# A two-layer encoder trunk: 28 projections stream the high and low halves of h side by side as 512 columns

## The chip, the cores and the metric

The kernel runs on one core of a Trainium2 chip. The metric is device time in microseconds, the median of several runs of the same program. TensorE does matrix products and writes PSUM; VectorE (DVE) and ScalarE (ACT) read and write SBUF and PSUM; GpSimd (POOL) does a few masks and roots; the DMA issues all stand in SyncE's queue (SP). Each engine takes its instructions strictly in the order in which they are written, and waits on semaphores of the others.

## The reference, cut to what matters

Each of two layers normalises x (256 rows of 1024), projects it by one wide matrix whose columns feed three branches, and merges the branches:

```
h = rmsnorm(x, norm_w)
proj = einsum('bld,de->ble', h, w_in)
(fq, fk, fv, ff, fg, sz, sxbc, sdt, dq, dk, dv, dg, mg) = split(proj)
y_a = forgetting_attention(fq, fk, fv, log_f) * silu(fg)
xbc = silu(causal_depthwise_conv(sxbc, conv_w, conv_b))   # 4 taps over time, by channel
y_b = rmsnorm(ssd_scan(xbc ...) * silu(sz)) * ssm_norm_w
y_c = rmsnorm(differential_attention(rope(dq), rope(dk), dv)) * silu(dg)
merged = sum over branches of sigmoid(mg) * (branch @ w_branch)
x = x + merged @ w_out
```

All of it is in float32. The kernel keeps that precision by writing each operand of a large product as the sum of two fp32r numbers, a high half and a low half, and adding three products: high by high, high by low, and low by high.

## The kernel before, in words

**Weights.** The columns are cut into chunks of 512 (`chunk_list`), each loaded as 4 units of 128 partitions by 1024 (two 128-row tiles k of 512 columns). `load_chunk` brings a unit in as `raw`; ScalarE casts it to `whi` (L231), VectorE subtracts to get `wlo` (L232). `whi` and `wlo` have 8 buffers each, so two chunks: the units of a chunk can only be split once TensorE has used up the same units two chunks earlier. A chunk is requested about two chunks ahead of its use.

**Two forms of product.** In the B form (`bform`, L249) h, or the output of a branch, is the stationary operand and the weights stream past, 512 columns at a time; the result has time on its partitions. In the A form (`aform`, L264) the weights are stationary and h streams past; the result has channels on its partitions and the 256 time steps along the bank. 14 chunks of each layer go in the A form: fq, fk and fg (two each, attention A), sB, sC, sx0, sx1 (the convolved part of branch B), dq and dk (two each, branch C). An A bank of 512 columns holds two tiles of 128 channels by 256 steps; for each of the 8 k-tiles and each of the two channel tiles there are three matmuls of 256 columns, with `whi` and the high half of h, `whi` and the low half, `wlo` and the high half.

**Emptying a bank.** `pp` has 3 PSUM banks for the large products. Each A chunk has a function that empties its bank: `t_evac` splits q and k straight from PSUM for the score products; `g_evac` computes u·(1+tanh(u/2)) from PSUM; `r_evac` copies dq and dk out with ScalarE (L766); `c_evac` copies with ScalarE into `sw` (L784), then ScalarE scales by the last tap (L470), VectorE adds three taps for each 128-channel tile (L473), ScalarE takes a tanh into the same buffer (L787) and VectorE multiplies (L788).

**Order.** Small pieces of the attention and the scan are jobs that `pump` places between the banks. The instructions of every engine are then ordered at compile time by a scheduler that follows priorities (earlier in the program first) and the buffers that are free; so the order on each engine is fixed before the run. `ap` is the pool of general SBUF buffers of 128 by 512, 41 of them; the halves of h take 8.

Of the kernel before, what the change touches and what calls it, by code (L numbers as in the profile page):

```python
# [24 lines left out]
KT = D // P  # L25
UNITS = 4
KU = KT // UNITS
# [69 lines left out]
def trunk(ctx: ExitStack, tc: tile.TileContext, x, norm_w, weights, small, vectors,  # L97
          final_norm_w, rope_t, out):
    nc = tc.nc
    V, S, G, PE = nc.vector, nc.scalar, nc.gpsimd, nc.tensor  # L100
# [1 line left out]
    const = ctx.enter_context(tc.tile_pool(name="const", bufs=1))  # L102
    wraw = ctx.enter_context(tc.tile_pool(name="wraw", bufs=4))
    wsp = ctx.enter_context(tc.tile_pool(name="wsp", bufs=8))
    ap = ctx.enter_context(tc.tile_pool(name="ap", bufs=41))
    sp = ctx.enter_context(tc.tile_pool(name="sp", bufs=5))
    tp = ctx.enter_context(tc.tile_pool(name="tp", bufs=2))
    sm = ctx.enter_context(tc.tile_pool(name="sm", bufs=2))
# [7 lines left out]
    def a2(shape=None, dtype=F32):  # L116
        return ap.tile(shape or [P, 2, 256], dtype, name="a2")
# [4 lines left out]
    def halves():  # L122
        return tuple([a2(dtype=F32R) for _ in range(4)] for _ in range(2))

    def at(half, kt):
        return half[kt // 2][:, kt % 2, :]

    def bank(pool, name):
        return pool.tile([P, 512], F32, name=name)
# [83 lines left out]
    chunks, _ = chunk_list()  # L213
# [36 lines left out]
                      start=((u, k, i) == order[0]), stop=((u, k, i) == order[-1]))  # L250
        return ps

    def aform(ch, act, jj):
        units, n = ch
        ahi, alo = act
        ps = bank(pp, "pp")
        for u in range(UNITS):
            whi, wlo = units[u]
            for k in range(KU):
                kt = u * KU + k  # L260
                for j in range(2):
                    c0 = (2 * jj + j) * P
                    for i, (w, a) in enumerate(((whi, ahi), (whi, alo), (wlo, ahi))):
                        PE.matmul(ps[:, j * T:(j + 1) * T], lhsT=w[:, k, c0:c0 + P], rhs=at(a, kt),  # L264
                                  start=(kt == 0 and j == 0 and i == 0), stop=(kt == KT - 1 and j == 1 and i == 2))
        return ps

    scr_x = dr.tile([2, P, D], F32, name="scr_x")
    L = [dict() for _ in range(DEPTH)]

    def make_h(l, tt, xt, xs, ss, gap):
        st = L[l]
        if tt == 0:
            st["hT"] = halves()
        with tc.high_priority(URGENT):
            r = norm_scale(ss)
            for c in range(2):
                norm_apply(xt, xs, r, st["nwb"], c)
        yield gap
        with tc.high_priority(URGENT):  # L280
            for c in range(2):
                st["split"] = split_rows(xs[c], st["hT"][0], st["hT"][1], tt, c)
        st[f"h{tt}"] = True
# [106 lines left out]
    def split_qk(key, src):  # L390
        tiles = [a2(dtype=F32R) for _ in range(2 if key[1] == "q" else 4)]
        (stack_q if key[1] == "q" else stack_k)(src, tiles)
        return tiles
# [323 lines left out]
    def plan(l):  # L717
        st = L[l]
# [36 lines left out]
            return f  # L755

        def t_evac(key):
            def f(jj, ps):
                st[f"{key[0:2]}{2 * int(key[2]) + jj}"] = split_qk(key, ps.rearrange("p (a t) -> p a t", t=T))
            return f  # L760

        def r_evac(key):
            def f(jj, ps):
                t = a2()
                st.setdefault("_" + key, []).append(t)
                S.copy(out=t, in_=ps.rearrange("p (a t) -> p a t", t=T))  # L766
                if jj == 1 and key[:2] == "dk":
                    start_job(rope, l, int(key[2]))
            return f

        def g_evac(key):
            def f(jj, ps):
                t = a2()
                p3 = ps.rearrange("p (a t) -> p a t", t=T)
                S.activation(out=t, in_=p3, func=AF.Tanh, scale=0.5)
                V.scalar_tensor_tensor(out=t, in0=t, scalar=1.0, in1=p3, op0=ALU.add, op1=ALU.mult)
                st[f"{key[0:2]}{2 * int(key[2]) + jj}"] = t
            return f

        def c_evac(key, j0):  # L780
            def f(jj, ps):
                t = a2()
                u = tp.tile([P, 2, T], F32, name="sw")
                S.copy(out=u, in_=ps.rearrange("p (a t) -> p a t", t=T))  # L784
                for i in range(2):
                    conv_tile(l, u[:, i, :], t[:, i, :], j0 + 2 * jj + i)
                S.activation(out=u, in_=t, func=AF.Tanh)  # L787
                V.scalar_tensor_tensor(out=t, in0=u, scalar=1.0, in1=t, op0=ALU.add, op1=ALU.mult)  # L788
                st.setdefault("_" + key, []).append(t)
                if jj == 1:  # L790
                    st[key] = st["_" + key]
            return f

        def merge(tt):
            if tt == 0:
# [159 lines left out]
    for idx, it in enumerate(items):  # L955
# [28 lines left out]
        for s in range(2):  # L984
            for (_, _, ch), ev in zip(got, it["evac"]):
                if it["kind"] == "A":
                    ev(s, aform(ch, it["act"](), s))
                else:
                    while f"{it['flag']}{s}" not in L[l]:
                        pump(100.0)  # L990
                    ev(s, bform(ch, it["act"](), s))
                pump(BUDGET)
# [27 lines left out]
```

## Time and profile before

| | |
|---|---|
| median of 3 runs | 955.47 us (955.02 to 956.32) |
| the profiled execution | 956.56 us, of which the span of the trace is 954.8 us |
| busy in the span | TensorE 942.0 us, weight loads 843.5 us, VectorE 700.9 us, ScalarE 599.3 us |
| share of the last-ending chain | TensorE 98% |

Busy time of an engine is the time in which an instruction of it is under way; matmuls overlap, so the mean duration of one is longer than the distance from one to the next. What a matmul costs in a stream is read from the chain in order of time, as length by count. The granted clock is given as a share of full speed, 1.00 for 2.4 GHz. Sums below are made against the profiled execution, 1.09 us over the median.

### The profile page before, as it was taken

Reading aid. Unit: us, or ns where it says so; the run is one execution under the profiler, and the core shown is the slowest. Engines: PE = TensorE matmul, PEld = TensorE weight load, DVE = VectorE, ACT = ScalarE, POOL = GpSimd, SP = SyncE. Lnnn points to the kernel's source line nnn. Section 1 sums busy time; section 2 is a strip of 40 time slices with the busy share of each in tenths; the row PEclk is TensorE's granted clock in tenths of the full one; section 3 lists DMA queues with packets and bytes.
Section 4 is the critical chain, followed back from the end, with each engine's and each line's share of the span. In section 5 each row is a group of like instructions: output and inputs, shape, how many; then the busy total and the mean of one; then the engine's idle time right before and its main releaser. Section 6 shows DMA issues by size and latency. Waiting matters only on the chain.

```text
span 954.8 us, 16246 instructions
## 1 busy us (share of the span) xinstructions
PE 942.0 (99%) x5924; PEld 843.5 (88%) x5924; DVE 700.9 (73%) x1434; ACT 599.3 (63%) x1141; POOL 36.3 (4%) x71
## 2 busy tenths in 40 slices
PE   7999999999999999999999999999999999999997
PEld 5999999988898988888889989898889999888885
DVE  5678677987667877864768768699777677797463
ACT  4668686654557868653546859566536596975442
POOL 1001100000000000100000110000000000010000
PEclk7999999999999999999999999999999999999999
DMA  6866634575555555555558664456645555555551
GB/s 231 263 219 198 206 101 166 159 226 154 177 189 181 182 190 179 151 171 194 193 181 271 209 206 134 132 172 191 201 143 194 174 186 186 188 158 162 177 188 44
DMA packets 60319, 172.45 MB, mean 181 GB/s; under 512 B 7312, under 2 KB 15824, under 8 KB 60240
## 3 DMA queue, kind: packets, MB, share of 16 engines
q1 hardware_dynamic: 60240, 171.43, 55.4%
q8 instruction: 46, 0.75, 0.3%
q14 instruction: 33, 0.27, 0.1%
HBM read 167.14 MB, written 2.16 MB: 177 GB/s over the span
## 4 chain that ended last, share of the span: by engine, by line
PE 98%; DMA 1%; DVE 1%; ACT 0%; SPq 0%; POOLq 0%; issue 0%
PE pp L249 51%; PE pp L264 34%; PE pq L400 2%; PE pt L457 2%; PE pq L583 1%; PE pq L401 1%; PE pq L447 1%; DMA raw<-in_weights_dram 1%; PE pt L627 1%; PE pt L198 1%; PE pt L458 1%; PE pq L692 1%; PE pq L590 0%; PE pt L700 0%; PE pq L499 0%; PE pt L699 0%
## 5 line engine op out<-in xcount | busy, mean ns | idle before, releaser
L249 PE MATMUL pp<-whi,a 128*128 128x512 f32 (+1 forms) x1472 | 452.5, 387 | 1.9 <-ACT a L188 1.1
L232 DVE TENSOR_TENSOR wlo<-raw,whi 128x1024 fp32r<-128x1024 f32 (+1 forms) x296 | 349.8, 1193 | 82.8 <-ACT whi L231 80.0
L231 ACT CAST whi<-raw 128x1024 fp32r<-128x1024 f32 (+1 forms) x296 | 302.2, 1027 | 135.2 <-PE pp L249 72.3
L264 PE MATMUL pp<-a,whi 128*128 128x256 f32 x1792 | 332.8, 284 | 0.0
L249 PEld LDWEIGHTS pp<-whi,a 128*128 128x128 f32 x1472 | 273.0, 189 | 55.3 <-ACT a L188 1.7
L264 PEld LDWEIGHTS pp<-a,whi 128*128 128x128 f32 x1792 | 281.5, 191 | 1.7 <-issue 1.4
L249 PE MATMUL pp<-wlo,a 128*128 128x512 f32 (+1 forms) x736 | 281.5, 385 | 0.0
L264 PE MATMUL pp<-a,wlo 128*128 128x256 f32 x896 | 255.2, 285 | 0.0
L264 PEld LDWEIGHTS pp<-a,wlo 128*128 128x128 f32 x896 | 171.5, 191 | 1.4 <-issue 1.4
L249 PEld LDWEIGHTS pp<-wlo,a 128*128 128x128 f32 x736 | 138.9, 189 | 25.8 <-DVE wlo L232 0.5
L183 POOL TENSOR_TENSOR rstd<-rstd,mhalf 128x2 f32<-128x2 f32 (+2 forms) x26 | 18.9, 727 | 760.6 <-DVE rstd L181 739.7
L473 DVE SCALAR_TENSOR_TENSOR a<-sw,pT,a 128x255 f32<-128x255 f32 (+2 forms) x96 | 41.8, 477 | 8.1 <-ACT a L470 7.9
L406 ACT ACTIVATE sc<-sc,dnm 128x128 f32<-128x128 f32 x64 | 28.6, 450 | 8.4 <-DVE dnm L403 8.3
L188 ACT CAST a<-pt 128x256 fp32r<-128x256 f32 x32 | 11.5, 371 | 33.2 <-PE pt L198 27.0
L400 PE MATMUL pq<-a,a 128*128 128x128 f32 (+1 forms) x128 | 31.8, 283 | 0.0
L809 DVE SCALAR_TENSOR_TENSOR a<-a,pp 128x512 f32<-128x512 f32 x24 | 16.4, 682 | 20.9 <-PE pp L249 20.9
L401 PE MATMUL pq<-a,a 128*128 128x128 f32 (+1 forms) x128 | 31.5, 269 | 0.0
L406 ACT ACTIVATE sc<-sc,nm 128x128 f32<-128x128 f32 (+1 forms) x64 | 28.5, 447 | 1.3 <-DVE nm L403 1.1
L400 PEld LDWEIGHTS pq<-a,a 128*128 128x128 f32 x128 | 23.7, 191 | 0.3
L401 PEld LDWEIGHTS pq<-a,a 128*128 128x128 f32 x128 | 23.6, 191 | 0.3
L403 DVE CUSTOM_DVE_ANT_0 sc<-pq,sc 128x128 f32<-128x128 f32 (+1 forms) x64 | 19.5, 351 | 5.9 <-POOL sc L426 4.9
L191 ACT ACTIVATE a<-pt,pT 128x256 fp32r<-128x256 f32 x32 | 14.9, 473 | 14.1 <-PE pt L627 12.4
(161 smaller groups left out, 842.6 us busy)
## 6 DMA issues: line engine op xcount, KB each, us to landing
raw<-in_weights_dram SPq DMA_DIRECT2D x280, 512.0 KB, 4.5
raw<-in_weights_dram SPq DMA_DIRECT2D x16, 272.0 KB, 3.5
sc<-scr SPq DMA_DIRECT2D x16, 256.0 KB, 5.5
a<-scr SPq DMA_DIRECT2D x16, 256.0 KB, 5.6
a<-in_x_dram SPq DMA_DIRECT2D x8, 256.0 KB, 5.2
sc<-scr SPq DMA_DIRECT2D x16, 128.0 KB, 5.2
a<-in_norm_w_dram SPq DMA_DIRECT2D x4, 256.0 KB, 6.5
rp<-a SPq DMA_DIRECT2D x32, 32.0 KB, 4.1
```

The source lines that it names most:

```text
L183: G.tensor_tensor(out=r[:, 0:width], in0=r[:, 0:width], in1=mhalf[:, 0:width], op=ALU.pow)
L231: S.copy(out=hi, in_=raw)
L232: V.tensor_tensor(out=lo, in0=raw, in1=hi.bitcast(F32), op=ALU.subtract)
L249: PE.matmul(ps[:, 0:n], lhsT=at(a, kt)[:, ts], rhs=w[:, k, 0:n], start=((u, k, i) == order[0]), stop=((u, k, i) == order[-1]))
L264: PE.matmul(ps[:, j * T:(j + 1) * T], lhsT=w[:, k, c0:c0 + P], rhs=at(a, kt), start=(kt == 0 and j == 0 and i == 0), stop=(kt == KT - 1 an ...
L400: PE.matmul(ps[:, o:o + n], lhsT=q[:, j, qs], rhs=k[:, j, 0:n], start=True, stop=False)
L401: PE.matmul(ps[:, o:o + n], lhsT=q[:, j, qs], rhs=kl[:, j, 0:n], start=False, stop=True)
L403: V.tensor_tensor_reduce(out=sc[:, sl], in0=ps[:, sl], in1=bias[:, sl], scale=-0.125, scalar=BIG, op0=ALU.add, op1=ALU.min, accum_out=nm[: ...
L406: S.activation(out=sc[:, sl], in_=sc[:, sl], func=AF.Exp, scale=-1.0, bias=nm[:, t:t + 1], accum_out=rs[:, t:t + 1])
L457: PE.matmul(po[r, 0:T], lhsT=v0, rhs=pTs[i][:, 0:T], start=True, stop=False)
L473: V.scalar_tensor_tensor(out=xc[:, s:T], in0=u[:, 0:T - s], scalar=pr["conv"](j, k), in1=xc[:, s:T], op0=ALU.mult, op1=ALU.add)
L809: V.scalar_tensor_tensor(out=t, in0=t, scalar=1.0, in1=ps, op0=ALU.add, op1=ALU.mult)
```

## The change

h's halves move from 8 buffers of `ap` into one tile `hboth`, where for each k-tile the 256 high columns and the 256 low columns lie side by side. An A bank now belongs to one tile of 128 channels: for each k-tile one matmul of 512 columns (`whi` against both halves) and one of 256 columns (`wlo` against the high half, added to the first half of the bank). The two halves of a finished bank are added by the new `fold`: ScalarE copies the second half to SBUF, VectorE adds the first half to it and writes one half of a pair buffer `u` (two buffers) or, for dq and dk, of a buffer of `ap`. After two banks the old work on a pair starts, reading the pair buffer in SBUF. The copies L766 and L784 go. `ap` shrinks from 41 to 30 buffers.

```
-    ap = ctx.enter_context(tc.tile_pool(name="ap", bufs=41))
+    ap = ctx.enter_context(tc.tile_pool(name="ap", bufs=30))
...
+    hboth = ctx.enter_context(tc.tile_pool(name="hp", bufs=1)).tile([P, KT, 2, T], F32R, name="hboth")
+    h_halves = tuple([hboth[:, 2 * i:2 * i + 2, s, :] for i in range(4)] for s in range(2))
...
-    def aform(ch, act, jj):
+    def aform(ch, j):
...
-                for j in range(2):
-                    c0 = (2 * jj + j) * P
-                    for i, (w, a) in enumerate(((whi, ahi), (whi, alo), (wlo, ahi))):
-                        PE.matmul(ps[:, j * T:(j + 1) * T], lhsT=w[:, k, c0:c0 + P], rhs=at(a, kt),
-                                  start=(kt == 0 and j == 0 and i == 0), stop=(kt == KT - 1 and j == 1 and i == 2))
+                kt, cols = u * KU + k, slice(j * P, (j + 1) * P)
+                PE.matmul(ps, lhsT=whi[:, k, cols], rhs=hboth[:, kt], start=(kt == 0), stop=False)
+                PE.matmul(ps[:, 0:T], lhsT=wlo[:, k, cols], rhs=hboth[:, kt, 0, :],
+                          start=False, stop=(kt == KT - 1))
...
+    def fold(ps, dst):
+        t = tp.tile([P, T], F32, name="fold")
+        S.copy(out=t, in_=ps[:, T:2 * T])
+        V.tensor_tensor(out=dst, in0=ps[:, 0:T], in1=t, op=ALU.add)
+
+    def raw_pair():
+        return tp.tile([P, 2, T], F32, name="u")
+
+    def folded(f, new=raw_pair):
+        pair = []
+
+        def g(j, ps):
+            if j % 2 == 0:
+                pair.append(new())
+            fold(ps, pair[-1][:, j % 2, :])
+            if j % 2:
+                f(j // 2, pair[-1])
+        return g
...
         def r_evac(key):
-            def f(jj, ps):
-                t = a2()
-                st.setdefault("_" + key, []).append(t)
-                S.copy(out=t, in_=ps.rearrange("p (a t) -> p a t", t=T))
+            def f(jj, u):
+                st.setdefault("_" + key, []).append(u)
...
-            return f
+            return folded(f, a2)
...
         def c_evac(key, j0):
-            def f(jj, ps):
+            def f(jj, u):
                 t = a2()
-                u = tp.tile([P, 2, T], F32, name="sw")
-                S.copy(out=u, in_=ps.rearrange("p (a t) -> p a t", t=T))
...
-                    ev(s, aform(ch, it["act"](), s))
+                    for j in (2 * s, 2 * s + 1):
+                        ev(j, aform(ch, j))
```

`t_evac` and `g_evac` are wrapped in `folded` in the same way and read `u` where they read the bank.

TensorE, inside an A bank of the kernel before (`a_152` and `a_149` are high halves of h, `a_156` and `a_153` low ones):

```order
228 L264 MATMUL pp<-a_152,whi 128x256
229 L264 MATMUL pp<-a_156,whi 128x256
230 L264 MATMUL pp<-a_152,wlo 128x256
231 L264 MATMUL pp<-a_152,whi 128x256
232 L264 MATMUL pp<-a_156,whi 128x256
233 L264 MATMUL pp<-a_152,wlo 128x256
```

The same work in the changed kernel, where L263 and L264 are the two matmuls of the new `aform`:

```order
112 L263 MATMUL pp<-hboth,whi 128x512
113 L264 MATMUL pp<-hboth,wlo 128x256
114 L263 MATMUL pp<-hboth,whi 128x512
115 L264 MATMUL pp<-hboth,wlo 128x256
116 L263 MATMUL pp<-hboth,whi 128x512
```

Three matmuls of 256 columns have become one of 512 and one of 256, and the two pairs of rows belong to the same bank where they belonged to two halves of it.

VectorE in layer 1 of the kernel before, at the first convolved chunk (sB): the taps of two pairs, with the splits of the weights that come two chunks later.

```order
850 L473 SCALAR_TENSOR_TENSOR a_7129<-sw,pT_3119,a_7129 128x255 x2
851 L473 SCALAR_TENSOR_TENSOR a_7129<-sw,pT_3119,a_7129 128x254 x2
852 L473 SCALAR_TENSOR_TENSOR a_7129<-sw,pT_3119,a_7129 128x253 x2
853 L788 SCALAR_TENSOR_TENSOR a_7129<-sw,a_7129 128x512
854 L473 SCALAR_TENSOR_TENSOR a_7215<-sw,pT_3119,a_7215 128x255 x2
855 L473 SCALAR_TENSOR_TENSOR a_7215<-sw,pT_3119,a_7215 128x254 x2
856 L232 TENSOR_TENSOR wlo<-raw,whi 128x1024
857 L473 SCALAR_TENSOR_TENSOR a_7215<-sw,pT_3119,a_7215 128x253 x2
858 L232 TENSOR_TENSOR wlo<-raw,whi 128x1024 x3
859 L788 SCALAR_TENSOR_TENSOR a_7215<-sw,a_7215 128x512
```

VectorE at the second and third convolved pairs of layer 1 in the changed kernel (`a_6747` and `a_6823` are their results; L492 are the taps, L802 the products, L235 the splits of weights, L271 the folds, L481 an attention output). Ahead of these rows stand the two folds that complete the pair of `a_6823`, then seven taps and one product of attention A.

```order
918 L492 SCALAR_TENSOR_TENSOR a_6747<-u,pT_2939,a_6747 128x253 x2
919 L492 SCALAR_TENSOR_TENSOR a_6823<-u,pT_2939,a_6823 128x254
920 L235 TENSOR_TENSOR wlo<-raw,whi 128x1024
921 L492 SCALAR_TENSOR_TENSOR a_6823<-u,pT_2939,a_6823 128x253
922 L235 TENSOR_TENSOR wlo<-raw,whi 128x1024
923 L481 TENSOR_TENSOR a_5447<-sc,a_5443 128x256
924 L492 SCALAR_TENSOR_TENSOR a_6823<-u,pT_2939,a_6823 128x253
925 L235 TENSOR_TENSOR wlo<-raw,whi 128x1024 x2
926 L802 SCALAR_TENSOR_TENSOR a_6747<-u,a_6747 128x512
927 L802 SCALAR_TENSOR_TENSOR a_6823<-u,a_6823 128x512
928 L271 TENSOR_TENSOR u<-pp,fold 128x256 x2
```

Where no instruction of VectorE stood between the end of a bank and its release before (ScalarE's copy freed it), the release of the next bank, the fold in row 928, now stands in VectorE's queue behind the taps of two pairs, four splits and two products.

## Rows read from the trace of the kernel before

**Rows 1.** The page: busy time, share of the span and instructions by engine.

```profile
PE 942.0 (99%) x5924; PEld 843.5 (88%) x5924; DVE 700.9 (73%) x1434; ACT 599.3 (63%) x1141; POOL 36.3 (4%) x71
```

**Rows 2.** The page: the chain that ended last, by engine.

```profile
PE 98%; DMA 1%; DVE 1%; ACT 0%; SPq 0%; POOLq 0%; issue 0%
```

**Rows 3.** The chain in order of time: start, length (us), what, how many.

```profile
237.52 24.75 PE pp L249 x109
...
262.27 17.27 PE pp L264 x144
```

**Rows 4.** Groups by shape, A-form matmuls: count | busy us, mean ns | idle before.

```profile
L264 PE MATMUL pp<-a,whi 128*128 128x256 f32 x1792 | 332.8, 284 | 0.0
...
L264 PE MATMUL pp<-a,wlo 128*128 128x256 f32 x896 | 255.2, 285 | 0.0
```

**Rows 5.** Groups by shape: copies and additions of the sizes that come and go.

```profile
L189 DVE TENSOR_TENSOR a<-pt,a 128x256 fp32r<-128x256 f32 x32 | 13.1, 419 | 11.7 <-ACT a L188 11.5
L188 ACT CAST a<-pt 128x256 fp32r<-128x256 f32 x32 | 11.5, 371 | 33.2 <-PE pt L198 27.0 <-DVE a L189 6.2
...
L766 ACT COPY a<-pp 128x512 f32<-128x512 f32 x16 | 9.3, 582 | 11.3 <-PE pp L264 11.1
...
L784 ACT COPY sw<-pp 128x512 f32<-128x512 f32 x16 | 9.3, 580 | 17.6 <-PE pp L264 17.3
```

**Rows 6.** Busy us by engine in four stretches, then granted clock, DMA share.

```profile
138.00:186.00 48.00, 48.00 (x381) 45.66 (x380) 40.05 (x68) 31.70 (x48) 0.00 (x0) 1.00 0.43 139
...
186.00:210.00 24.00, 24.00 (x119) 20.21 (x118) 23.64 (x51) 13.27 (x21) 0.00 (x0) 1.00 0.78 238
210.00:262.00 52.00, 52.00 (x255) 43.75 (x254) 36.99 (x69) 24.94 (x43) 1.02 (x1) 1.00 0.55 169
507.00:650.00 143.00, 143.00 (x1167) 137.28 (x1166) 113.57 (x262) 102.18 (x198) 7.67 (x16) 1.00 0.53 177
```

**Rows 7.** VectorE's timeline: start, length, instruction, count [idle before].

```profile
592.60 2.36 DVE L232 TENSOR_TENSOR wlo<-raw,whi 128x1024 fp32r<-128x1024 f32 x2
...
615.84 2.45 DVE L473 SCALAR_TENSOR_TENSOR a<-sw,pT,a 128x255 f32<-128x255 f32 x6
619.04 0.69 DVE L788 SCALAR_TENSOR_TENSOR a<-sw,a 128x512 f32<-128x512 f32 x1 [0.76 <-ACT sw L787]
```

**Rows 8.** Waits in 138 to 186 us: us in total, times, longest.

```profile
ACT sw L784 <- PE pp L264: 6.4, 2, 3.6
ACT whi L231 <- PE pp L264: 5.8, 10, 2.4
DVE a L473 <- ACT a L470: 3.9, 3, 1.8
...
DVE wlo L232 <- ACT whi L231: 1.6, 2, 1.2
DVE a L788 <- ACT sw L787: 0.8, 1, 0.8
```

**Rows 9.** Timeline of the start, ScalarE and TensorE.

```profile
14.17 0.37 ACT L188 CAST a<-pt 128x256 fp32r<-128x256 f32 x1 [0.54 <-DVE a L189]
14.44 1.99 ACT L231 CAST whi<-raw 128x1024 fp32r<-128x1024 f32 x2
...
15.54 2.08 PE L249 MATMUL pp<-whi,a 128*128 128x512 f32 x4 [0.80 <-ACT whi L231]
16.33 0.42 ACT L942 ACTIVATE a<-a 128x256 f32<-128x256 f32 x1
```

**Rows 10.** Busy us by engine at the start, then granted clock, DMA share.

```profile
0.00:15.50 15.50, 9.62 (x38) 7.45 (x38) 5.33 (x13) 5.49 (x12) 2.36 (x14) 0.83 0.77 280
15.50:41.00 25.50, 25.43 (x148) 22.73 (x149) 18.37 (x36) 17.23 (x36) 0.56 (x1) 0.90 0.69 212
```

More of the change, by code (lines that the diff above doesn't have):

```diff
@@ L251, in bform @@
         return ps
-    def aform(ch, act, jj):
+    def aform(ch, j):
         units, n = ch
-        ahi, alo = act
         ps = bank(pp, "pp")
@@ L259, in aform @@
             for k in range(KU):
-                kt = u * KU + k
-                for j in range(2):
-                    c0 = (2 * jj + j) * P
-                    for i, (w, a) in enumerate(((whi, ahi), (whi, alo), (wlo, ahi))):
-                        PE.matmul(ps[:, j * T:(j + 1) * T], lhsT=w[:, k, c0:c0 + P], rhs=at(a, kt),
-                                  start=(kt == 0 and j == 0 and i == 0), stop=(kt == KT - 1 and j == 1 and i == 2))
-        return ps
+                kt, cols = u * KU + k, slice(j * P, (j + 1) * P)
+                PE.matmul(ps, lhsT=whi[:, k, cols], rhs=hboth[:, kt], start=(kt == 0), stop=False)
+                PE.matmul(ps[:, 0:T], lhsT=wlo[:, k, cols], rhs=hboth[:, kt, 0, :],
+                          start=False, stop=(kt == KT - 1))
+        return ps
+    def fold(ps, dst):
[13 more added lines that the diff above has]
+        return g
     scr_x = dr.tile([2, P, D], F32, name="scr_x")
@@ L273, in make_h @@
         if tt == 0:
-            st["hT"] = halves()
+            st["hT"] = h_halves
         with tc.high_priority(URGENT):
@@ L757, in t_evac, with f @@
         def t_evac(key):
-            def f(jj, ps):
-                st[f"{key[0:2]}{2 * int(key[2]) + jj}"] = split_qk(key, ps.rearrange("p (a t) -> p a t", t=T))
-            return f
+            def f(jj, u):
+                st[f"{key[0:2]}{2 * int(key[2]) + jj}"] = split_qk(key, u)
+            return folded(f)
         def r_evac(key):
-            def f(jj, ps):
-                t = a2()
-                st.setdefault("_" + key, []).append(t)
-                S.copy(out=t, in_=ps.rearrange("p (a t) -> p a t", t=T))
+            def f(jj, u):
+                st.setdefault("_" + key, []).append(u)
                 if jj == 1 and key[:2] == "dk":
                     start_job(rope, l, int(key[2]))
-            return f
+            return folded(f, a2)
         def g_evac(key):
-            def f(jj, ps):
+            def f(jj, u):
                 t = a2()
-                p3 = ps.rearrange("p (a t) -> p a t", t=T)
-                S.activation(out=t, in_=p3, func=AF.Tanh, scale=0.5)
-                V.scalar_tensor_tensor(out=t, in0=t, scalar=1.0, in1=p3, op0=ALU.add, op1=ALU.mult)
+                S.activation(out=t, in_=u, func=AF.Tanh, scale=0.5)
+                V.scalar_tensor_tensor(out=t, in0=t, scalar=1.0, in1=u, op0=ALU.add, op1=ALU.mult)
                 st[f"{key[0:2]}{2 * int(key[2]) + jj}"] = t
-            return f
+            return folded(f)
         def c_evac(key, j0):
-            def f(jj, ps):
+            def f(jj, u):
                 t = a2()
-                u = tp.tile([P, 2, T], F32, name="sw")
-                S.copy(out=u, in_=ps.rearrange("p (a t) -> p a t", t=T))
                 for i in range(2):
@@ L791, in f @@
                     st[key] = st["_" + key]
-            return f
+            return folded(f)
         def merge(tt):
```

## The prediction

> **What bounds the kernel now.** I read the busy shares first, then the chain that ended last, then the waits of the stretch that the change loads most. TensorE is busy 942.0 of 954.8 us [rows 1] and the chain runs through it for 98% [rows 2]; in the stretches from 138 us on in the table it is busy for the whole of each, at a granted clock of 1.00 [rows 6]. So a nanosecond taken out of TensorE's stream is a nanosecond of the span, as long as the other engines keep up, and a stall of TensorE is lost in full. The A-form matmuls never waited (idle 0.0 before both groups, [rows 4]).
>
> What a matmul costs is the distance to the next one. In the chain, 144 matmuls of 256 columns took 17.27 us, 119.9 ns each, and 109 of 512 columns took 24.75 us, 227.1 ns each [rows 3]. The 256 further columns cost 107.1 ns, so each matmul carries 119.9 − 107.1 = 12.8 ns that don't depend on its columns.
>
> The second engine to watch is VectorE, 73% busy overall [rows 1] but not evenly: 40.05 of 48 us at the convolved chunks of layer 0, then 23.64 of 24 us, then 36.99 of 52 us [rows 6].
>
> **What the change takes away.** 14 chunks × 2 layers × 4 channel tiles × 8 k-tiles = 896 groups. A group was 3 × 119.9 = 359.8 ns and becomes 227.1 + 119.9 = 347.0 ns. The columns are the same 768; one matmul's fixed 12.8 ns goes. 896 × 12.8 ns = **−11.5 us**, all of it on the path. The trace holds no stream that alternates 512 and 256 columns with stationary weights; the two prices come from separate streams. The bounds for this term are 0 (the fixed part stays) and 11.5; I take 11.5, because the same fixed part fits both streams.
>
> A rule of the Trainium skill speaks against this. The Trainium skill, "TensorE: Matmul & The Clock Gate", section "Back-to-back issue gap", gives the gap of a matmul on its own as N/2.4 plus 2.5 ns at the full clock. By it the removed matmuls would give back only 896 × 2.5 ns, an estimate of 2.2 us. This trace differs: 12.8 ns against 2.5 [rows 3], and the measurement decides.
>
> **What the change adds off the path.** Each of 112 banks now needs a ScalarE copy of 256 columns, near 371 ns, and a VectorE addition of 256 columns from PSUM, near 419 ns [rows 5]. VectorE gets 112 × 0.42 = 47 us and rises to 748 of some 950, 79%. ScalarE gets 112 × 0.371 = 41.6 us and loses 32 copies of 0.58 us (16 of L766 and 16 of L784, [rows 5]), 18.6 us, so 23 more: 622 us, 65%. As totals both hide beside TensorE's 942.
>
> Locally they don't. In layer 1's ten A chunks VectorE would have 113.57 + 40 × 0.42 = 130.4 us of work [rows 5, 6] in 143 − 320 groups × 0.0128 = 138.9 us, 94%. At the convolved chunks of layer 0 it has 40.05 + up to 16 × 0.42 = 46.8 us in about 46.4, and right behind it 23.64 in 24 [rows 6]: full for 72 us, with room only in the 52 us that follow. What covers this is the weight buffers' lead of about a chunk (some 11 us) and three PSUM banks.
>
> **The wait that it brings.** A bank lasts 8 × 0.347 = 2.78 us where it lasted 48 × 0.1199 = 5.76. With three buffers, a bank must be empty two banks after its end: 5.6 us instead of 11.5. Before, ScalarE alone freed the convolved banks. Now VectorE's fold does, and it stands in VectorE's queue behind what the order shows. The units of the next weights but one become free during the fourth bank of a chunk, so four splits come in a burst, usually ahead of the fourth fold. And the pair tile `u` has two buffers, so the first fold of a pair waits for the last product (L802) of the pair two before; with `sw` it was ScalarE's copy that had this wait, and the bank had twice the time.
>
> I cost the two worst places. Layer 1, at sC: between its second and third fold stand 12 taps at 2.45/6 = 0.41, 4 splits at 2.36/2 = 1.18, 2 products at 0.69 [rows 7], two attention instructions and the fold itself at about 0.42 [rows 5]: 4.9 + 4.7 + 1.4 + 1.2 = 12.2 us. The second fold can be done at the earliest 0.37 + 0.42 = 0.8 us after its bank; the third is needed three banks later, so VectorE has 8.3 − 0.8 = 7.5 us. TensorE stalls **4.7 us**. What is queued behind the fold is the next fold and the taps, so one such stall covers both. Layer 0, same place one pair later: 10 taps, 4 splits, 2 products, one fold, 10.6 us, against two A banks and one B bank (24 × 0.2271 = 5.45) less 0.8, so 10.2: **0.4 us**. The other folds with a burst ahead have 5 to 8 us of VectorE work in the order by the same prices; they fit in 7.5 us and the small products between, or miss by tenths.
>
> These sums let VectorE run without a gap. In 138 to 186 us it waited for ScalarE 3.9 + 1.6 + 0.8 = 6.3 of 48 us, 13% [rows 8]; 13% of 12.2 + 10.6 us adds **3.0 us**. The bounds of this term are 0 (VectorE late means ScalarE is ahead) and 13% of all 130.4 us of both layers, 34 us; I take the two bursts only, since elsewhere a wait still fits into the idle time: ScalarE itself sat waiting for TensorE 6.4 + 5.8 us in the same 48 [rows 8].
>
> **Edits that I cost at nothing.** The scheduler also moves the squares of x's second half (L942) on ScalarE from behind two casts to between the splits of the first half: four of about 0.6 us with their read-out, 2.4 us ahead of the cast at 14.44 us that TensorE waits for at 15.54 [rows 9]. They no longer stand between later casts, where x's second half is also needed. Bounds: 2.4 lost, 1 won; I take 0. The smaller pool loses 11 buffers, of which h's halves used 8; the missing three could hold back a load, 0 to 2 us; I take 0, since the lead of the loads covers it. Pairs read from SBUF instead of PSUM cost about the same. The clock reads 1.00 everywhere after the start and 0.83 and 0.90 only where TensorE had gaps [rows 6, 10]; I take no loss there, with the stalls short.
>
> **Sum.** −11.5 + 4.7 + 0.4 + 3.0 = −3.4 us. On the profiled execution's 956.56 that is 953.2; the median of the runs lies 1.09 lower, 955.47 − 3.4 = **952.1 us**.
>
> **The rivals.** *The gain in full*: VectorE's bursts fit because the fixed order was made with them, and the 13% wait is slack. For it: VectorE already ran 98% full in 186 to 210 us without a stall of TensorE [rows 6]. Against: the 12.2 us in 7.5. Time 955.47 − 11.5 = 944.0, or 946 with small stalls.
>
> *Slower, by the fourth fold*: at each of the 28 chunks four splits stand ahead of a fold, about 6.7 us of VectorE work in a budget near 8.0 us (7.5 and small products), 1.3 us to spare. If VectorE waits for ScalarE's casts for a share w of the burst, each chunk loses 6.7w − 1.3. It decides when 28 times that passes 11.5 + 1.9 us, at 0.48 us a chunk, w = 27%. Measured is 13% [rows 8], but folds add a hand-over from ScalarE each, and ScalarE has 23 us more to do. At w = 30%: 28 × 0.71 = 20, so 955.47 − 11.5 + 20 = 964. It would also bring clock losses.
>
> *A draw*: stalls of 9.6 to 13.4 us, by the two places above and a few tenths at some twenty other bursts. Time 953.6 to 957.4.
>
> *The fixed part stays*: the 12.8 ns is not paid per matmul but comes with each stream's weight loads and columns, and a stream of 512 and 256 keeps the time of three 256. Then nothing is won and 8.1 lost: 963.6. Nothing in the rows speaks for it; both streams show the same fixed part [rows 3]. The Trainium skill's rule above lies close to it; by its 2.5 ns the time would be 961, an estimate.
>
> **How the numbers follow.** Two runs of this kernel differ by about 0.14%, so 0.2% (1.9 us) is what can be told from no change. Chances: the forecast (946 to 953.5) 0.39, the gain in full 0.13, a draw 0.22, slower by the fourth fold 0.24, the fixed part 0.02. So faster 0.52, same 0.22, slower 0.26. The likeliest is 952; its own range is 947 to 955. To leave out no more than 2 in 10, the range reaches to the full gain, 944, and towards the slower rival, to 962.
>
> **What the profile after should show.** A chain in which a pair of A matmuls takes 347 ns: if it takes 357 or more, the first term failed. TensorE idle before L263 or its weight load, some 8 us in all, released by VectorE's fold, most of it near 575 us (sC of layer 1): if idle is under 2 us the burst sum was too high; if it lies at every chunk the slower rival holds. VectorE about 748 us busy, ScalarE 622. A granted clock under 1.00 after 41 us would mean that stalls cost more than their length. The prediction fails above all if VectorE's gaps in the attention chunks, which I read as slack, are waits that the fold inherits.

## The result and the profile after

The changed kernel takes 986.69 us (median of 5 runs, 983.43 to 988.85) where the kernel before takes 955.47: a ratio of 1.0322 [1.0303, 1.0341], 31 us slower, and outside the range of 944 to 962 us. The profiled execution's span is 985.0 us, 30.2 more than before.

The page of the changed kernel, busy time by engine and the chain by engine; they answer to [rows 1, 2].

```profile
PE 953.0 (97%) x5028; PEld 799.2 (81%) x5028; DVE 735.1 (75%) x1546; ACT 616.3 (63%) x1221; POOL 37.8 (4%) x71
...
PE 68%; DVE 11%; DMA 8%; ACT 7%; issue 5%; SPq 1%; POOL 0%; POOLq 0%; DVEq 0%; ACTq 0%
```

Neither VectorE nor ScalarE came near its limit: 735 and 616 us, less than the 748 and 622 forecast. But TensorE's share of the chain fell from 98% to 68%, and it is idle for 985.0 − 953.0 = 32.0 us where it was idle for 12.8. That is 19.2 of the 30.2 us.

Busy us by engine in five stretches, then granted clock, DMA share and GB/s; they answer to [rows 6].

```profile
186.00:240.00 54.00, 51.61 (x257) 43.23 (x256) 44.74 (x102) 23.25 (x36) 0.00 (x0) 0.97 0.57 185
...
340.00:400.00 60.00, 56.05 (x269) 45.74 (x268) 42.63 (x99) 41.41 (x94) 3.16 (x5) 0.97 0.50 158
...
610.00:660.00 50.00, 47.34 (x279) 39.59 (x278) 44.22 (x95) 32.99 (x71) 0.00 (x0) 0.97 0.44 137
...
833.00:890.00 57.00, 52.88 (x255) 43.32 (x254) 42.23 (x105) 39.80 (x98) 4.15 (x6) 0.94 0.48 146
890.00:985.00 95.00, 88.08 (x409) 72.27 (x407) 52.85 (x79) 40.07 (x71) 2.51 (x4) 0.98 0.43 143
```

These are the stretches in which TensorE had gaps; in the others of the same table from 60 us on the clock reads 1.00. At the start it is the other way round: against 0.83 and 0.90 in the kernel before [rows 10] the changed kernel shows

```profile
0.00:15.50 15.50, 8.55 (x38) 6.47 (x38) 5.65 (x15) 6.73 (x19) 2.88 (x15) 0.89 0.79 282
15.50:41.00 25.50, 25.13 (x158) 22.66 (x159) 20.29 (x37) 18.09 (x32) 0.03 (x1) 1.00 0.76 254
```

By the clock records of the two traces TensorE was busy at the lower level, 1.2 GHz, for 19.2 us in all, 16.2 of them after 60 us; before it was for 8.4 us, all at the start. A 512-column matmul at the start of the changed kernel took 427 ns at that level and 231 to 236 at the upper one, so nearly half of such time is lost: about 7 us after 60 us, about 5 net of the start. (The shares of the five stretches, 1.6 + 1.8 + 1.5 + 3.4 + 1.9 = 10.2 us, are more, as they count low clock in idle time too.) With the idle time that makes 24 of the 30.2 us. The other 6 are busy time at the full clock: the stream of matmuls, which was to give 11.5 us back, gave nothing. Part of these 6 are short waits, since a matmul counts as busy to its modelled end.

What TensorE waited for in the whole span: us in total, times, longest.

```profile
PE pp L252 <- ACT a L773: 3.3, 2, 1.6
...
PE pt L526 <- DVE a L802: 2.6, 1, 2.6
PE pq L419 <- DVE wlo L235: 2.4, 2, 1.2
PE pt L547 <- DVE a L802: 2.4, 1, 2.4
PE pp L263 <- DVE u L271: 2.0, 4, 1.0
...
PE pq L420 <- ACT a L407: 1.9, 4, 0.7
PE pp L263 <- DVE a L271: 1.5, 2, 0.8
```

Only the lines of L263 are the wait that the prediction costed, for a bank that VectorE's fold must empty: 3.5 us. The weight loads ahead of these matmuls wait a little longer, 5.6 us:

```profile
PEld pp L263 <- DVE u L271: 3.6, 6, 1.2
...
PEld pp L263 <- DVE a L271: 2.0, 2, 1.0
```

Of the others, four lines are waits of TensorE's small work for what is computed *from* a folded bank: L526 and L547 (transposes of the state-space part) for the convolved tiles of L802, L419 and L420 (scores) for the splits of q and k that follow rope. The first line is a wait for a bank of the mg chunks that ScalarE's tanh (L773) must empty; the pool experiment below shows how it hangs on the scores.

The start of a chunk in each profile, less its start in the kernel before (us, from the TensorE timelines; .0 and .1 are the layers). The columns after the first are experiments told below.

```
         changed  layout  pool30  no add  both mends  GpSimd  two copies
mg00.0     -2.7    -3.9    -3.3    -5.8       1.5       9.5      -2.6
wb01.0      2.5    -3.4    -2.8    -4.5       4.1      10.6       6.0
mg10.0      5.0    -2.3    -1.8    -3.3       8.6      11.8       7.1
wb11.0     11.8    -1.8     4.6    -3.2       9.6      11.8       7.1
mg00.1     16.2    -3.2     3.5    -6.5      17.0      21.7       5.9
wb01.1     17.1    -2.6     4.1    -4.8      19.2      22.8      14.7
mg10.1     21.3    -1.6     5.1    -3.6      23.4      24.0      16.3
wb11.1     29.6    -1.0    10.6    -3.5      23.7      24.0      16.5
end        30.2    -0.5    11.2    -2.9      24.3      24.6      17.1
```

The largest single loss stands between mg10 and wb11, 6.8 and 8.3 us in the two layers: a place of which the prediction doesn't speak. Between it and the last rope projection, dk1, lie the two chunks dg0 and dg1.

VectorE at the end of dk1 in layer 0 and the rope behind it (start, length, instruction).

```profile
339.15 4.63 DVE L235 TENSOR_TENSOR wlo<-raw,whi 128x1024 fp32r<-128x1024 f32 x4 [0.84 <-ACT whi L234]
343.70 0.41 DVE L271 TENSOR_TENSOR a<-pp,fold 128x256 f32<-128x256 f32 x1
...
350.36 0.74 DVE L671 STREAM_SHUFFLE sw<-rp 128x512 f32<-128x512 f32 x1
351.00 1.21 DVE L235 TENSOR_TENSOR wlo<-raw,whi 128x1024 fp32r<-128x1024 f32 x1
352.12 0.68 DVE L672 TENSOR_TENSOR sw<-sw,rot 128x512 f32<-128x512 f32 x1
352.73 0.68 DVE L673 TENSOR_TENSOR rp<-rp,rot 128x512 f32<-128x512 f32 x1
353.33 2.35 DVE L235 TENSOR_TENSOR wlo<-raw,whi 128x1024 fp32r<-128x1024 f32 x2
355.60 0.68 DVE L674 TENSOR_TENSOR rp<-rp,sw 128x512 f32<-128x512 f32 x1
```

The last fold of dk1 stands behind four weight splits. ScalarE's copy for it stands behind their four casts in the same way, from 341.88 to 342.24. The gathering transfers of rope start after the fold, the shuffle at 350.36, and three more splits stand between rope's own four instructions, so its last addition ends at 356.3. In the kernel before, the shuffle began at 342.1 and the last addition ended at 345.4. TensorE itself was 5 us behind at this point; rope was 8 to 11 behind.

### The profile page after: what moved, and what is told of

It reads as the page before. It is cut to its first block, busy times and chain, and to the rows that moved or that the text cites. A ratio compares the mean times of both kernels' runs of the same rounds, so it can differ in the third digit from the quotient of the medians.

```text
span 985.0 us, 14723 instructions
## 1 busy us (share of the span) xinstructions
PE 953.0 (97%) x5028; PEld 799.2 (81%) x5028; DVE 735.1 (75%) x1546; ACT 616.3 (63%) x1221; POOL 37.8 (4%) x71
## 4 chain that ended last, share of the span: by engine, by line
PE 68%; DVE 11%; DMA 8%; ACT 7%; issue 5%; SPq 1%; POOL 0%; POOLq 0%; DVEq 0%; ACTq 0%
PE pp L252 35%; PE pp L263 15%; PE pp L264 8%; DVE wlo L235 5%; ACT whi L234 2%; DMA rp<-a 2%; DMA a<-rp 2%; PE pt L476 1%; PE pq L602 1%; DMA sc<-scr 1%; PE pq L466 1%; DMA raw<-in_weights_dram 1%; ACT sc L425 1%; DVE sc L422 1%; DMA a<-in_x_dram 1%
## 5 line engine op out<-in xcount | busy, mean ns | idle before, releaser
L235 DVE TENSOR_TENSOR wlo<-raw,whi 128x1024 fp32r<-128x1024 f32 (+1 forms) x296 | 348.1, 1193 | 78.0 <-ACT whi L234 76.2
L263 PE MATMUL pp<-hboth,whi 128*128 128x512 f32 x896 | 324.2, 400 | 3.6 <-DVE u L271 2.0
L252 PE MATMUL pp<-whi,hboth 128*128 128x512 f32 (+1 forms) x960 | 296.0, 388 | 5.6 <-ACT a L773 3.3
L264 PE MATMUL pp<-hboth,wlo 128*128 128x256 f32 x896 | 254.0, 283 | 0.0
L252 PEld LDWEIGHTS pp<-whi,hboth 128*128 128x128 f32 x960 | 178.3, 191 | 43.8 <-ACT a L773 3.6
L263 PEld LDWEIGHTS pp<-hboth,whi 128*128 128x128 f32 x896 | 168.9, 188 | 43.7 <-DVE u L271 3.6
L252 PE MATMUL pp<-wlo,hboth 128*128 128x512 f32 (+1 forms) x480 | 184.5, 387 | 0.0
L264 PEld LDWEIGHTS pp<-hboth,wlo 128*128 128x128 f32 x896 | 168.7, 188 | 1.4 <-issue 1.0
L252 PE MATMUL pp<-whi,a 128*128 128x512 f32 x512 | 165.1, 398 | 0.0
L252 PEld LDWEIGHTS pp<-whi,a 128*128 128x128 f32 x512 | 96.4, 189 | 20.3 <-DVE a L823 0.6
L252 PE MATMUL pp<-wlo,a 128*128 128x512 f32 x256 | 101.2, 395 | 0.0
L492 DVE SCALAR_TENSOR_TENSOR a<-u,pT,a 128x255 f32<-128x255 f32 (+2 forms) x96 | 41.9, 474 | 1.6 <-ACT a L489 1.5
L419 PE MATMUL pq<-a,a 128*128 128x256 f32 (+1 forms) x128 | 33.6, 287 | 3.9 <-DVE wlo L235 2.4
L271 DVE TENSOR_TENSOR u<-pp,fold 128x256 f32<-128x256 f32 x80 | 32.2, 415 | 2.8 <-ACT fold L270 2.4
L420 PE MATMUL pq<-a,a 128*128 128x128 f32 (+1 forms) x128 | 32.1, 269 | 1.9 <-ACT a L407 1.9
L823 DVE SCALAR_TENSOR_TENSOR a<-a,pp 128x512 f32<-128x512 f32 x24 | 16.4, 683 | 23.4 <-PE pp L252 23.4
```

What stands on the lines that cost most here:

```text
L235: V.tensor_tensor(out=lo, in0=raw, in1=hi.bitcast(F32), op=ALU.subtract)
L252: PE.matmul(ps[:, 0:n], lhsT=at(a, kt)[:, ts], rhs=w[:, k, 0:n], start=((u, k, i) == order[0]), stop=((u, k, i) == order[-1]))
L263: PE.matmul(ps, lhsT=whi[:, k, cols], rhs=hboth[:, kt], start=(kt == 0), stop=False)
L264: PE.matmul(ps[:, 0:T], lhsT=wlo[:, k, cols], rhs=hboth[:, kt, 0, :], start=False, stop=(kt == KT - 1))
L271: V.tensor_tensor(out=dst, in0=ps[:, 0:T], in1=t, op=ALU.add)
L419: PE.matmul(ps[:, o:o + n], lhsT=q[:, j, qs], rhs=k[:, j, 0:n], start=True, stop=False)
```

## The experiments

All times are medians; "before" ran beside each and stayed between 955.5 and 956.5 us.

**What the form gains, and what the tile of h costs.** The first kernel changes only where h is kept:

```diff
+ h_halves = tuple([hboth[:, 2 * i:2 * i + 2, s, :] for i in range(4)] for s in range(2))
- st["hT"] = halves()          (ap, bufs=41)
+ st["hT"] = h_halves          (ap, bufs=33)
```

> The kernel before with h's halves in the one tile hboth and 33 buffers in ap, everything else old. Theory A (a matmul of 512 columns that reads hboth takes 233 ns instead of 227, wherever it stands): the B-form chunks on h go from 227 to 233 ns per matmul, some 1250 of them, +8 us; the A-form matmuls of 256 columns go from 120 to 118 ns, 2688 of them, -5 us; together 956 to 964. Theory B (the 233 ns come with the new form or its neighbours): 227 and 120 ns as before, 954 to 957.

957.6 us, ratio 1.0017 [1.0007, 1.0026]. Its chain in order of time (start, length, what, how many), to be held against [rows 3]:

```profile
234.15 25.39 PE pp L252 x109
259.55 16.96 PE pp L267 x144
```

With no change of form, a 512-column matmul with a slice of h stationary now takes 25.39/109 = 232.9 ns instead of 227.1, and a 256-column one that streams h takes 117.8 instead of 119.9. That is +5.8 ns × 1248 = +7.3 us and −2.1 ns × 2688 = −5.6 us. In the changed kernel the first price stays and the second has little left to act on. Its chain has the same 25.39 us, and its pairs take 353 ns where nothing stands between (29 of them from 271.72 to 281.97):

```profile
239.99 25.39 PE pp L252 x109
...
271.72 0.40 PE L263 MATMUL pp<-hboth,whi 128*128 128x512 f32 x1
...
281.97 0.39 PE L263 MATMUL pp<-hboth,whi 128*128 128x512 f32 x1
```

At this place of the tile, three old matmuls cost 3 × 117.8 = 353.4 ns, nearly the same. The next two kernels and a third put the tile elsewhere in SBUF, by allocating it ahead of the weights' buffers: the changed kernel, the old form, and the changed kernel without additions (its fold is one ScalarE copy of the first half; the second half is left out).

```diff
+ hboth = ctx.enter_context(tc.tile_pool(name="hp", bufs=1)).tile([P, KT, 2, T], F32R, name="hboth")
  wraw = ctx.enter_context(tc.tile_pool(name="wraw", bufs=4))
```

> The changed kernel with the tile of h allocated ahead of the weights' buffers, so that it lies at another place in SBUF; nothing else is changed. Theory A, the 233 ns of a 512-column matmul that reads h hang on where the tile lies: back to 227 ns, 2150 matmuls by 6 ns less, 972 to 976 us. Theory B, they hang on how the tile is laid out (512 columns of one index side by side): 233 ns stay, 984 to 989 us.

> The kernel before, its matmuls in the old form, with h in the one tile, allocated ahead of the weights' buffers, and 33 activation buffers. Theory A, place sets the price: matmuls with h stationary at 227 ns as before, 256-column ones that stream h at 117 ns instead of 120, 2688 by 3 ns less, 8 us: 946 to 950 us, faster than both kernels with no change of form. Theory B, the 117 ns belong to the pairing of 512 and 256 columns: 954 to 957 us.

> The changed kernel with the tile of h ahead of the weights' buffers, whose fold is ScalarE's copy of the first half alone (the second half is left out). It shows what the form could give without a fold. Theory A: at this place a pair takes 233 + 117 = 350 ns against 3 x 117 = 351 ns of the old form, so it comes out within 2 us of the old form with the tile there, 945 to 950 us. Theory B, the form does gain once nothing waits: 5 us or more under the old form there, below 943 us.

982.1, 956.0 and 948.6 us. The chain of the old form with the tile at the other place:

```profile
237.19 24.75 PE pp L252 x109
261.94 17.27 PE pp L267 x144
```

To the last digit it has the lengths of [rows 3]: place sets the price, not layout, and the 118 ns go as the 233 do. So I was wrong to expect 946 to 950 there; what the one stream gains the other loses (957.6 and 956.0). Against 956.0 the kernel without additions has 948.6: here the form is worth 7.4 us. It falls into theory A's range of times, but by luck: A had the old form at 946 to 950 too. That the form gains is theory B's point, at a higher time than B's 943. In the changed kernel with the tile there, the matmuls with h stationary took 227 ns again, but most of that was lost to longer waits: 982.1 against 986.7, between its two theories.

**The addition.** With the tile where the changed kernel has it:

```diff
- t = tp.tile([P, T], F32, name="fold")
- S.copy(out=t, in_=ps[:, T:2 * T])
- V.tensor_tensor(out=dst, in0=ps[:, 0:T], in1=t, op=ALU.add)
+ S.copy(out=dst, in_=ps[:, 0:T])
```

> The changed kernel, but the fold leaves the second half of the bank out: ScalarE copies the first half to the pair, VectorE does nothing. So ScalarE frees the bank and VectorE has 47 us less. If the folds' place in VectorE's queue is the cause of the stalls, they go: the stream's gain of 0 to 8 us stays, 947 to 957. If the rope chain is late for another reason (its transfers, ScalarE's order, the smaller pool), most of the loss stays, above 970.

954.4 us, ratio 0.9986 [0.9976, 0.9995]. The column "no add" of the table stays ahead of the kernel before throughout; its largest step back is 1.7 us. So the 32 us between 954.4 and 986.7 hang on the second step of the fold, VectorE's, with the order that the compiler makes around it. Against the layout kernel, 957.6 us, the form is worth 3.2 us with the tile at this place.

**Where: rope's projections alone, and all but them.** dq and dk in the old form with ScalarE's copy, the rest changed; then the reverse, on the layout kernel with 32 activation buffers.

```diff
- if it["kind"] == "A":
+ if it["kind"] == "A" and it["key"][:2] in ("dq", "dk"):
+     ev(s, aform_old(ch, it["act"](), s))
+ elif it["kind"] == "A":
```

> The changed kernel, but the eight chunks dq and dk keep the old form and ScalarE's copy out of the bank. Theory R (the rope chain behind dk1 starts late because its pair is folded late, and TensorE waits at the scores in the mg chunks of branch B): about 20 of the 31 us come back, less 2 us of stream, so 967 to 971. Rival F (every chunk loses its share by its folds): 8 of 28 chunks, some 9 us, 976 to 980.

> The kernel before with hboth, and the new form with folds for the chunks dq and dk alone (ap has 32 buffers). Theory R (the rope chain is where most is lost): 955 plus 20 plus what the layout costs (0 to 8), 973 to 983. Rival F (each chunk its share): 955 plus 9 plus 0 to 8, 962 to 972.

978.4 and 967.0 us, both in rival F's range. Both lose, so rope is one place among several. The first was the surprise: with rope's projections in the old form it still lost 6.6 and 5.6 us between mg10 and wb11. Something there did not come from the fold.

**The smaller pool.** In the program order of that kernel, the last of the four k splits behind the second rope waits for a buffer. The layout kernel with its pool cut to the 30 buffers of the changed one does the same (ScalarE's row for this split, first with 33 buffers, then with 30; behind it stands what it waits for):

```diff
- ap = ctx.enter_context(tc.tile_pool(name="ap", bufs=33))
+ ap = ctx.enter_context(tc.tile_pool(name="ap", bufs=30))
```

```
358 L388 CAST a_4191<-a_4010 64x512 [waits DMAHW3_49,Activation_49]
375 L388 CAST a_4191<-a_4010 64x512 [waits PE_49]
```

> The kernel before with h in the one tile (the first experiment, 957.6 us), and its activation pool cut from 33 to the 30 buffers that the changed kernel has; all projections in the old form. In the program order the last of the four k splits of the second rope then waits for a buffer that TensorE still reads, which with 33 it does not. Theory P, the pool alone makes the loss between mg10 and wb10: 5 to 9 us per layer there, 967 to 976 us in all. Theory Q, the late buffer is covered unless VectorE is late too (the kernel without additions has 30 buffers and loses 1.2 us there): 957 to 961 us.

966.6 us, ratio 1.0111 [1.0093, 1.013]: 9.0 us over the layout kernel, for three buffers, with every matmul in the old form. Theory P holds: 6.4 and 5.5 us are lost from mg10 to wb11 in the two layers, and the time is just under its 967. ScalarE and TensorE of this kernel at the place (start, length, instruction [idle before, and what ended it]):

```profile
369.18 2.95 ACT L234 CAST whi<-raw 128x1024 fp32r<-128x1024 f32 x3
372.16 0.61 ACT L388 CAST a<-a 64x512 fp32r<-64x512 f32 x1
372.80 0.62 ACT L390 CAST a<-a 64x512 fp32r<-64x512 f32 x1
...
374.33 0.57 ACT L747 ACTIVATE a<-pp 128x512 f32<-128x512 f32 x1
374.81 0.58 ACT L757 ACTIVATE a<-pp 128x512 f32<-128x512 f32 x1
...
373.47 0.33 PE L403 MATMUL pq<-a,a 128*128 128x128 f32 x1 [1.73 <-ACT a L390]
...
375.44 0.79 PE L252 MATMUL pp<-whi,hboth 128*128 128x512 f32 x1 [1.12 <-ACT a L757]
```

The buffer itself is free in time: ScalarE takes the split up at once at 372.16. What costs is its *place*. The order is fixed ahead, and as the buffer was reckoned to come free late, the split was put 17 rows further down, behind five more weight casts, the last three of them right ahead of it. The score at L403 waits for it, TensorE stands, the tanh of the next banks stands behind it on ScalarE and holds those banks, and TensorE waits again. In the kernel without additions the late split was put ahead of those casts, and with the same 30 buffers it lost 0.1 us from mg10 to wb11: the price of a short pool is set by where the order puts the late instruction.

The changed kernel with 32 buffers, won by folding in place and by one scratch tile for rope:

```diff
- ap ... bufs=30   ;   sw = tp.tile(..., name="sw")
+ ap ... bufs=32   ;   sw = tp.tile(..., name="sw", bufs=1)
- t = tp.tile(...); S.copy(out=t, in_=ps[:, T:2 * T]); V.tensor_tensor(out=dst, in0=ps[:, 0:T], in1=t, ...)
+ S.copy(out=dst, in_=ps[:, T:2 * T]); V.tensor_tensor(out=dst, in0=ps[:, 0:T], in1=dst, ...)
```

> The changed kernel with 32 activation buffers: the fold writes ScalarE's copy into its destination and adds in place, so the fold tile goes, and rope's scratch tile has one buffer. No k split waits for a buffer of TensorE. Theory P, the pool makes the loss between mg10 and wb10: it falls from 8 to 9 us per layer to under 3, 970 to 975 us in all. Theory R, the late start of the second rope (its last fold behind four weight splits on VectorE) makes it: 983 to 988 us.

981.0 us, between the two theories. From mg10 to wb11 it now loses 3.0 and 1.3 us instead of 6.8 and 8.3, as P says, but it loses 7 us more up to mg00 of layer 0 (it starts mg00 4.6 us late, where the changed kernel was 2.7 ahead), in an order that the edit had also changed.

**Two banks at a time, and both mends.** The same matmuls, with the passes over the weights shared by two banks; then this with the 32 buffers.

```diff
- for j in (2 * s, 2 * s + 1): ev(j, aform(ch, j))
+ for j, ps in aform_pair(ch, s): ev(j, ps)      # both banks open, k-tile by k-tile
```

> The changed kernel, but two banks of a chunk are filled together, pass by pass over the weights (the same matmuls, two banks open at a time). Theory W: in the changed kernel the weights of a chunk come free only within its last bank, 2.8 us, instead of 5.7 us, so the four splits of the next chunk come in one burst and the last fold stands behind them; here they come 1.4 us apart again, the second rope starts 3 to 4 us sooner, 972 to 980 us in all. Rival: the burst is not what makes the rope late, and two banks that end together queue their folds: 984 to 992 us.

> The changed kernel with both mends: two banks filled together, and 32 activation buffers (fold in place, one scratch tile for rope). If the late k split and the burst of weight splits are separate losses, their gains add: 986.7 less 5.7 less 8.8, 969 to 975 us. Rival, both act through the same wait of TensorE in mg10 and mg11: 976 to 981 us.

977.9 and 977.1 us. The first lies in theory W's range, yet not for its reason. VectorE of that kernel at the same place:

```profile
338.38 4.64 DVE L235 TENSOR_TENSOR wlo<-raw,whi 128x1024 fp32r<-128x1024 f32 x4 [0.77 <-ACT whi L234]
342.93 0.42 DVE L273 TENSOR_TENSOR a<-pp,fold 128x256 f32<-128x256 f32 x1
...
349.29 0.74 DVE L673 STREAM_SHUFFLE sw<-rp 128x512 f32<-128x512 f32 x1
```

The four splits are still in one piece, the fold is still behind them, and the shuffle is 1 us sooner, as is TensorE itself. W has fallen. The traces show where the pairing won: from mg10 to wb11 this kernel loses 3.9 and 1.6 us instead of 6.8 and 8.3, and ScalarE's last k split there ends 18.4 us after the start of mg10 where it ended 23.4 us after it in the changed kernel (15.3 with 32 buffers, 8.6 in the kernel before, all in layer 0). So the pairing too seems to win by an earlier place of this split in the order. Both mends win at the same spot and don't add, as the rival had it.

**Which engine, and how many steps.** First the addition from SBUF, on GpSimd and on VectorE, with 31 buffers and one scratch tile for rope, and GpSimd's with the tile at the other place:

```diff
+ S.copy(out=dst, in_=ps[:, 0:T])
  S.copy(out=t, in_=ps[:, T:2 * T])
- V.tensor_tensor(out=dst, in0=ps[:, 0:T], in1=t, op=ALU.add)
+ G.tensor_tensor(out=dst, in0=dst, in1=t, op=ALU.add)      # or V
```

> The changed kernel, with the addition taken off VectorE: ScalarE copies both halves of a bank to SBUF and GpSimd, which is busy 4% of the span, adds them; 31 activation buffers, so that no k split waits for one. Nothing is left out. Theory V, VectorE's additions in its full queue make the loss that the pool does not: 955 to 962 us, near the 954.4 of the kernel without additions. Rival L, one step more between a bank and its readers costs this whichever engine takes it: 970 to 980 us.

> As the kernel with GpSimd's addition, but VectorE adds, from SBUF, so that it no longer holds a bank. Theory B, TensorE's waits for banks that VectorE holds make the loss: 955 to 965 us. Theory V, the place of the additions in VectorE's order makes it (rope, convolution and heads get their inputs late), and the banks are a small part, the 3.5 us of waits before L263: 974 to 984 us.

> As the kernel with GpSimd's addition, with the tile of h ahead of the weights' buffers, where the matmuls with h stationary took 227 ns again instead of 233. Theory A, with VectorE's stalls gone the whole gain of this reaches the end: 7 to 8 us below the kernel with GpSimd's addition, 947 to 955 us, under the kernel before. Rival, something else moves and eats it, as with VectorE's addition (982 against 987): within 3 us of the kernel with GpSimd's addition.

978.0, 991.3 and 975.2 us. With VectorE relieved of every addition the time is in rival L's range, not in V's. But it is not the same loss that stayed. By the table nothing is lost from mg10 to wb11 any more; instead the kernel with GpSimd's addition loses 9.5 us up to mg00 of layer 0 and 9.9 from wb11 to the next mg00, where the changed kernel had gained 2.7 and lost 4.4. So what VectorE's addition and the pool cost behind rope did go, and the longer fold, with a second ScalarE copy and GpSimd's step, cost as much in the attention A and convolution chunks. TensorE's two longest waits there are again for readers of folded banks:

```profile
PE pt L527 <- DVE a L803: 5.8, 2, 2.9
PE pq L420 <- ACT a L407: 5.6, 2, 2.8
```

With VectorE adding from SBUF TensorE waits 0.5 us before A-form matmuls instead of 3.5, and the kernel is the slowest of all, above both theories' ranges: held banks were not the main loss. GpSimd's kernel with the tile at the other place is 2.8 us faster than without, as its rival had it. Next the third buffer of the pair tile, on the kernel with both mends:

```diff
- return tp.tile([P, 2, T], F32, name="u")            (ap, bufs=32)
+ return tp.tile([P, 2, T], F32, name="u", bufs=3)    (ap, bufs=31)
```

> The kernel with two banks filled together and 32 activation buffers (977.1 us), with three buffers of the pair tile in place of two and 31 activation buffers. Theory U, the third pair waits for a buffer that the convolution of the first still uses, and TensorE's 4.9 us of waits for that fold, with the lower clock behind them, go: 969 to 973 us. Theory V, the fold stands behind the convolutions in VectorE's order whatever the buffers: 975 to 979 us.

979.1 us, at the edge of theory V's range and far from U's. The wait for this fold was 4.9 us with two buffers and is 4.2 us with three, so in that kernel they don't make it. Last, the number of steps alone (both leave out the second half of each bank):

```diff
  two copies:   S.copy(out=t, in_=ps[:, 0:T]); S.copy(out=dst, in_=t)
  vector copy:  V.tensor_copy(dst, ps[:, 0:T])
```

> The changed kernel with a fold of two steps on ScalarE, none on VectorE: the first half of a bank is copied to a tile and from there to its destination (the second half is left out). Theory V, VectorE's queue makes the loss: 955 to 962 us, near the kernel with one copy (954.4 us). Theory L, each step more between a bank and its readers lets TensorE's later work wait, whichever engine takes it: 968 to 980 us, as with GpSimd's addition (978 us).

> The changed kernel with a fold of one step on VectorE, none on ScalarE: VectorE copies the first half of a bank to its destination (the second half is left out). Theory V: the step stands in VectorE's order as the addition did, 970 to 982 us. Theory L: one step, as ScalarE's one copy, 955 to 964 us.

973.3 and 963.4 us. Both are in theory L's ranges. With one step on ScalarE the time is 954.4 in all, one on VectorE 9.0 more, two on ScalarE 18.9 more with VectorE doing nothing for the fold, one on each 32.3 more. A second step costs more here (18.9 and 23.3) than a change of engine (9.0 and 13.4), but it isn't steps alone: three with GpSimd take less (978.0) than two with VectorE (986.7, or 981.0 with 32 buffers). A step added is also 112 more instructions in the order of an engine, and no run tells the two apart.

## Why the prediction was wrong

**The stream, −11.5 us.** Failed. The step was that the 12.8 ns belong to each matmul and that h's new tile costs nothing to read. A pair takes 352.8 ns (347.0 predicted) on the mean of the 767 pairs, of 802 that follow each other, that took under 420 ns; the others waited. 359.8 − 352.8 = 7.0 ns × 896 = −6.3 us. And the 1248 matmuls with h stationary, which the prediction doesn't count among what is touched, take +7.3 us. Together +1 us. With the tile at the other place, where its readers take their old times, the form gave 7.4 us, so there the mechanism was right, with two thirds of its size. The Trainium skill, "TensorE: Matmul & The Clock Gate", section "Back-to-back issue gap", with its 2.5 ns for a matmul on its own would have the gain at 2.2 us, an estimate. By the kernels without additions the runs show 2.3 ns a group at one place (353.4 against 351.1) and 9.4 ns at the other (359.8 against 350.4): the Trainium skill's figure is near the one and far from the other.

**The stall before L263, 4.7 + 0.4 + 3.0 us.** Right in kind, but not at the places costed: 3.5 us of idle matmuls and 5.6 us of idle weight loads in all, none of it at sC of layer 1, where 4.7 us were forecast (sC begins at 613 us in the kernel before and 620 in the changed one, not near 575). That `u`'s two buffers bring it about isn't borne out: a third buffer, tried on the kernel with both mends, took 0.7 of 4.9 us off.

**The pool, costed at 0 with a bound of 2 us.** Failed: 9.0 us by itself in the old form, and 5.7 us came back with 32 buffers in the changed kernel. The step said that the lead of the loads covers three missing buffers. It was no load that was held back, but a split that feeds TensorE.

**The clock, no loss.** Failed: behind TensorE's waits, of up to 2.6 us, the clock fell, which cost about 7 us after 60 us. A start with less time at the lower level gave some 2 of them back.

**What was left out, the largest part.** This is the step that failed most: the fold's effect on whatever reads its result was put at nothing, without a reason. The prediction asked, for each fold, when its bank is free, and gave the rival "slower by the fourth fold" a price by the same question. The fold did stand behind four splits, at dk1 as the rival has it. But the banks were little of what TensorE waited for. The fold is a step in the way of everything that reads the bank: rope's transfers, then its splits, then the scores; the convolution, then the transposes. Before, these began after one ScalarE copy. TensorE's small work has a fixed place among its matmuls, so it meets late inputs there and stops the stream. The sum of it all was 32 us by the kernel without additions.

What stays open: with the pool mended and the addition off VectorE, 978.0 − 956.2 = 22 us over the kernel before remain, at other places than the changed kernel's largest loss. That time grows with the steps between bank and reader is shown by the kernels with one and two steps; whether by the delay of the readers or by the engines' fuller queues is not, nor which reader costs how much, as every edit also made a new order. No version with the whole computation beat the kernel before.

## What to carry to other kernels

Where one in-order engine bounds the kernel and takes in side work at fixed places, cost a new step in an evacuation by its readers: follow the chain from the bank to the next instruction of the bounding engine, and see how much lead it had. In a program whose order is fixed ahead, a few buffers taken from a pool can cost as much as an instruction added to every bank (9.0 us each here); compare what instructions wait for in the two orders, above all a new wait for the bounding engine's buffers. And when a tile moves, count every reader of it, not those of the edit alone.

## What the runs showed of the hardware that was not expected

The time of a matmul hung on where in SBUF the tile lies that it reads. The same old-form program with the same layout of h took 227.1 ns (h stationary, 512 columns) and 119.9 ns (h streamed, 256 columns) with the tile ahead of the weights' buffers, and 232.9 and 117.8 ns with it behind the other pools. In the program with 232.9 ns the 512-column matmuls whose stationary operand lies in `ap` kept 227 ns. What in the address makes the difference was not tried; moving the tile ahead also moves the other pools.
